# A fused LayerNorm and GELU on one core: the last row's store moved from the hand-written section to a Tile DMA behind it

## Chip, core and metric

One core of a Trainium2 chip. The metric is the device time of one execution in microseconds (us), the median of several runs; lower is better. The profile of one execution comes beside it.

## The reference, cut

```python
def reference(x, gamma, beta, eps):            # x: 8 x 1024 x 2048 float32
    mean = np.mean(x, axis=-1, keepdims=True)
    var = np.var(x, axis=-1, keepdims=True)
    out = gamma * (x - mean) / np.sqrt(var + eps) + beta
    return (0.5 * out * (1 + np.tanh(np.sqrt(2 / np.pi) * (out + 0.044715 * out ** 3)))).astype(np.float32)
```

67 MB come in and 67 MB go out; there is no other large traffic.

## The kernel before

The 8192 rows of 2048 are cut into 16 batches (B) of 128 partitions by 4 rows (R). From here on "a row" of a batch is one of these 4, that is 128 rows of x, one per partition, 1 MB. Five buffers `xts` hold batches in flight. Within one section, `tile_critical`, every engine has its own block and its own semaphores: SyncE (SP) loads batches, VectorE (DVE) takes statistics and scales by gamma, GpSimd (POOL) takes the power for the standard deviation, TensorE adds beta in PSUM, ScalarE (ACT) normalises, applies GELU in place and issues the stores. ACT stores a whole batch at a time, but the last batch row by row, so that its first rows do not wait for the fourth.

```python
    def by_row(b):
        return b == B - 1
    def stored(b):                      # count of the slot's store semaphore before batch b
        return sum(16 * (R if by_row(c) else 1) for c in range(b) if slot(c) == slot(b))

    with tc.tile_critical(no_gpsimd_drain=True):
        with nc.Block(no_gpsimd_drain=True) as block:
            ...
            @block.scalar
            def _(ac):
                ...
                for t in range(T + 1):
                    ...                                     # normalise tile t into yks
                    ins = ac.activation(out=xt[:, q], in_=pss[i % 2], func=ACT.Gelu_apprx_tanh)._wait_ge(s_t, i + 1)
                    if by_row(b):
                        ins.then_inc(s_r, 1)
                        ac.dma_start(out=og[b, :, q:q + 1], in_=xt[:, q:q + 1])._wait_ge(
                            s_r, b + q + 1).then_inc(s_store[slot(b)], 16)
                        ac.sem_inc(s_g, 1)
                    ...
        # still in the section: GpSimd waits for every store
        for b in range(B, B + SLOTS):
            nc.gpsimd.wait_ge(s_store[slot(b)], stored(b))
```

Behind the block stands a barrier of all engines, then GpSimd's waits, then the exit of the section, then the two closing handshakes of the program.

Of the kernel before, what the change touches and what calls it, by code (L numbers as in the profile page):

```python
# [10 lines left out]
R = 4  # L11
# [5 lines left out]
def kernel(  # L17
# [8 lines left out]
    nc = tc.nc  # L26
# [7 lines left out]
    T = n // P  # L34
    B = T // R
    assert (B - 1) % SLOTS == 0
    xg = xf.rearrange("(b p r) d -> b p r d", p=P, r=R)
    og = of.rearrange("(b p r) d -> b p r d", p=P, r=R)
# [7 lines left out]
    def sb(name, shape, dt):  # L46
        return pool.tile(shape, dt, name=name)

    xts = [sb(f"xt{s}", [P, R, d], f32) for s in range(SLOTS)]
# [17 lines left out]
    def sem(name):  # L67
        return tc.alloc_semaphore(name)
# [3 lines left out]
    s_store = [sem(f"store{s}") for s in range(SLOTS)]  # L72
# [15 lines left out]
    def slot(b):  # L88
        return (b + SLOTS - 1) % SLOTS

    def row(p):
        return rows[p:p + 1, :, :d // K]

    def split(v):
        return v.rearrange("o (k f) -> o k f", k=K)
# [4 lines left out]
    def by_row(b):  # L100
        return b == B - 1

    def stored(b):
# [5 lines that stand above are left out]
            @block.sync  # L109
            def _(sy):  # L110
                for b in range(B):
                    s = slot(b)
                    if stored(b):
                        sy.wait_ge(s_store[s], stored(b))
                    for q in range(R):
                        if b == 0:
                            sy.dma_start(out=xts[s][:, q:q + 1], in_=xg[0, :, q:q + 1]).then_inc(s_first[q], 16)
                    if b:
                        sy.dma_start(out=xts[s], in_=xg[b]).then_inc(s_load[s], 16)
# [68 lines left out]
            @block.scalar  # L188
            def _(ac):
                ac.preload_act_table(ACT.Gelu_apprx_tanh)  # L190
                for k, (p, src) in enumerate(((64, gamma), (0, beta), (32, beta))):
                    ac.dma_start(out=row(p), in_=src.rearrange("(o k f) -> o k f", o=1, k=K)).then_inc(s_par[k], 16)
                ac.wait_ge(s_m, 1)
                ac.activation(out=split(b_hl[0:1]), in_=row(0), func=ACT.Identity)._wait_ge(s_par[1], 16).then_inc(s_c, 1)  # L194
                ac.activation(out=split(b_hl[32:33]), in_=row(32),  # L195
                              func=ACT.Identity)._wait_ge(s_par[2], 16).then_inc(s_c, 1)
                ac.activation(out=g_t, in_=pss[0], func=ACT.Identity)._wait_ge(s_tg, 1).then_inc(s_c, 1)  # L197
                for t in range(T + 1):
                    if t < T:
                        b, q = divmod(t, R)  # L200
                        ac.activation(out=yks[t % 2], in_=xts[slot(b)][:, q], func=ACT.Identity, scale=rss[:, q:q + 1],  # L201
                                      bias=nms[:, q:q + 1])._wait_ge(s_p, t + 1).then_inc(s_n, 1)
                    i = t - 1
                    if i < 0:
                        continue
                    b, q = divmod(i, R)
                    xt = xts[slot(b)]
                    ins = ac.activation(out=xt[:, q], in_=pss[i % 2], func=ACT.Gelu_apprx_tanh)._wait_ge(s_t, i + 1)  # L208
                    if by_row(b):
                        ins.then_inc(s_r, 1)  # L210
                        ac.dma_start(out=og[b, :, q:q + 1], in_=xt[:, q:q + 1])._wait_ge(  # L211
                            s_r, b + q + 1).then_inc(s_store[slot(b)], 16)
                        ac.sem_inc(s_g, 1)
                    elif q == R - 1:
                        ins.then_inc(s_r, 1)
                        ac.dma_start(out=og[b], in_=xt)._wait_ge(s_r, b + 1).then_inc(s_store[slot(b)], 16)  # L216
                        ac.sem_inc(s_g, 1)
                    else:
                        ins.then_inc(s_g, 1)
# [29 lines left out]
                    pe.sem_inc(s_z, -R)  # L249


        for b in range(B, B + SLOTS):
            nc.gpsimd.wait_ge(s_store[slot(b)], stored(b))


# [1 line left out]
_INS = ['x', 'gamma', 'beta', 'eps']  # L257
_OUTS = [((8, 1024, 2048), 'float32')]
# [30 lines left out]
```

## Time and profile before

| what | value | where read |
|---|---|---|
| median time | 319.69 us, 3 runs, 319.49 to 319.76 | timing |
| span of the profiled execution | 317.8 us | head of the page |
| busiest compute engine | DVE, 265.0 us, 83% | part 1 of the page |
| DMA engines, loads and stores | 49.4% + 49.1% | part 3 of the page |
| last activation ends | 305.29 us | timeline |
| last store issued / landed | 305.32 / 316.50 us | trace |
| from last landing to the end | 1.29 us | difference to the span |

The digits of the DMA row are tenths of all 16 DMA engines' time in 1/40 of the span: a row of nines next to TensorE, ScalarE and VectorE at 77 to 83% (GpSimd 25%) says that the transfers set the pace. "PEq", "ACTq", "POOLq" and "SPq" are an engine's sequencer, where waits, no-ops, branches and issues of DMA stand; they are not counted as busy. A store has "landed" with the last of its 16 semaphore increments; a "ring" is what one DMA engine still has to do for one queue; a "straggler" is a DMA engine that is late against the others. The lines themselves are in the prediction.

### The profile page before, as it was taken

Reading aid. Unit: us, or ns where it says so; the run is one execution under the profiler, and the core shown is the slowest. Engines: PE = TensorE matmul, PEld = TensorE weight load, DVE = VectorE, ACT = ScalarE, POOL = GpSimd, SP = SyncE. Lnnn points to the kernel's source line nnn. Section 1 sums busy time; section 2 is a strip of 40 time slices with the busy share of each in tenths; the row PEclk is TensorE's granted clock in tenths of the full one; section 3 lists DMA queues with packets and bytes.
Section 4 is the critical chain, followed back from the end, with each engine's and each line's share of the span. In section 5 each row is a group of like instructions: output and inputs, shape, how many; then the busy total and the mean of one; then the engine's idle time right before and its main releaser. Section 6 shows DMA issues by size and latency. Waiting matters only on the chain.

```text
span 317.8 us, 2075 instructions
## 1 busy us (share of the span) xinstructions
PE 244.3 (77%) x520; PEld 57.1 (18%) x520; DVE 265.0 (83%) x514; ACT 253.9 (80%) x132; POOL 79.0 (25%) x73
## 2 busy tenths in 40 slices
PE   2769988888888898888877868598595895868810
PEld 1211222111212122211111111122121111112100
DVE  3499999999999999999969799696996969879500
ACT  2679999999999999999969779696995969968920
POOL 1033323232323231323213222231312213212000
DMA  7999999999999999999999999999999999999994
GB/s 291 438 462 396 459 396 445 412 454 404 458 400 459 422 437 445 412 450 408 458 417 441 437 421 454 404 458 412 450 433 425 450 408 450 408 458 421 437 404 206
DMA packets 5571, 134.27 MB, mean 423 GB/s; under 512 B 656, under 2 KB 704, under 8 KB 704
## 3 DMA queue, kind: packets, MB, share of 16 engines
q1 hardware_dynamic: 2736, 67.11, 49.4%
q10 hardware_dynamic: 2832, 67.13, 49.1%
q14 instruction: 3, 0.02, 0.0%
HBM read 67.13 MB, written 67.11 MB: 422 GB/s over the span
## 4 chain that ended last, share of the span: by engine, by line
DMA 44%; DVE 27%; ACT 19%; PE 3%; issue 2%; ACTq 1%; DVEq 0%; SPq 0%
DMA out_dram<-xt 27%; DVE sts L148 15%; DMA xt<-in_x_dram 15%; ACT yk L201 12%; DVE zg L164 9%; ACT xt L208 7%; PE ps L226 2%; DMA rows<-in_gamma_dram 2%; DVE mvs L157 2%; DVE nms L141 1%; ACTq L216 1%; DVE ves L158 1%; PE ps L243 1%; ACT g_t L197 1%; ACTq L211 0%
## 5 line engine op out<-in xcount | busy, mean ns | idle before, releaser
L148 DVE BATCH_NORM_STATS2 sts<-xt 128x6 f32<-128x512 f32 x256 | 163.5, 681 | 23.7 <-DMA xt<-in_x_dram 21.7
L201 ACT ACTIVATE yk<-xt,nms,rss 128x2048 bf16<-128x2048 f32 x64 | 134.1, 2095 | 41.7 <-DVE nms L141 41.2
L243 PE MATMUL ps<-zg,ident 128*128 128x512 bf16 x256 | 120.8, 627 | 50.9 <-DVE zg L164 50.9
L132 POOL TENSOR_TENSOR rss<-ves,mhalf 128x1 f32<-128x1 f32 x64 | 78.0, 1219 | 216.5 <-DVE ves L158 157.0
L239 PE MATMUL ps<-b_hl,ones_b 33*128 33x512 bf16 x256 | 120.6, 624 | 2.2 <-PEq L234 2.2
L208 ACT ACTIVATE xt<-ps 128x2048 f32<-128x2048 f32 x64 | 118.8, 1857 | 1.5 <-PE ps L243 1.5
L164 DVE TENSOR_TENSOR zg<-yk,g_t 128x2048 bf16<-128x2048 bf16 x64 | 78.0, 1218 | 5.0 <-ACT yk L201 3.0
L243 PEld LDWEIGHTS ps<-zg,ident 128*128 128x128 bf16 x256 | 27.6, 130 | 144.1 <-DVE zg L164 108.7
L239 PEld LDWEIGHTS ps<-b_hl,ones_b 33*128 33x128 bf16 x256 | 27.0, 127 | 92.1 <-issue 88.4
L157 DVE BATCH_NORM_AGGREGATE mvs<-sts 128x2 f32<-128x24 f32 x64 | 16.9, 264 | 2.2
L141 DVE TENSOR_SCALAR nms<-mvs,rss 128x1 f32<-128x1 f32 x64 | 12.6, 196 | 0.0
L226 PE MATMUL ps<-rows,ones 1*128 1x512 f32 x8 | 7.2, 1072 | 6.0 <-DMA rows<-in_gamma_dram 6.0
L158 DVE TENSOR_SCALAR ves<-mvs 128x1 f32<-128x1 f32 x64 | 9.8, 154 | 2.2
L194 ACT ACTIVATE b_hl<-rows 1x2048 bf16<-1x2048 f32 x1 | 1.9, 1909 | 4.9 <-DMA rows<-in_beta_dram 4.9
L226 PEld LDWEIGHTS ps<-rows,ones 1*128 1x128 f32 x8 | 2.5, 323 | 9.2 <-DMA rows<-in_gamma_dram 6.0
L172 DVE TENSOR_TENSOR b_hl<-rows,b_hl 1x2048 bf16<-1x2048 f32 x1 | 2.3, 2281 | 2.1 <-ACT b_hl L195 2.1
L197 ACT ACTIVATE g_t<-ps 128x2048 bf16<-128x2048 f32 x1 | 1.9, 1877 | 2.4 <-PE ps L226 2.4
L190 ACT ACT_TABLE_LOAD x1 | 1.3, 1283 | 0.9 <-SPq L106 0.9
L167 DVE MEMSET b_hl<- 33x1024 uint32 x1 | 0.9, 912 | 1.2 <-SPq L106 1.2
L195 ACT ACTIVATE b_hl<-rows 1x2048 bf16<-1x2048 f32 x1 | 1.9, 1908 | 0.0
L123 POOL MEMSET ones<- 65x128 f32 x1 | 0.2, 202 | 0.5 <-SPq L106 0.5
L127 POOL TENSOR_SCALAR_AFFINE_SELECT ident<-ident 128x128 bf16<-128x128 bf16 x1 | 0.3, 294 | 0.1
(7 smaller groups left out, 0.9 us busy)
## 6 DMA issues: line engine op xcount, KB each, us to landing
xt<-in_x_dram SPq DMA_DIRECT2D x15, 4096.0 KB, 24.3
out_dram<-xt ACTq DMA_DIRECT2D x15, 4096.0 KB, 37.0
xt<-in_x_dram SPq DMA_DIRECT2D x4, 1024.0 KB, 8.1
out_dram<-xt ACTq DMA_DIRECT2D x4, 1024.0 KB, 12.7
rows<-in_beta_dram ACTq DMA_DIRECT2D x2, 8.0 KB, 5.6
rows<-in_gamma_dram ACTq DMA_DIRECT2D x1, 8.0 KB, 5.0
```

The costliest lines, as they stand in the source:

```text
L132: po.tensor_tensor(out=rss[:, c], in0=ves[:, c], in1=mhalf, op=ALU.pow)._wait_ge(s_a, k + 1).then_inc(s_q, 1)
L141: ve.tensor_scalar(out=nms[:, c], in0=mvs[:, q, 0:1], scalar1=rss[:, c], scalar2=-1.0, op0=ALU.mult, op1=ALU.mult)._wait_ge(s_q, count).th ...
L148: ins = ve.bn_stats(out=sts[:, q, j, :], in_=xr[:, j, :])
L157: ve.bn_aggr(out=mvs[:, q], in_=sts[:, q])._wait_ge(s_o, count + 1).then_inc(s_o, 1)
L158: ve.tensor_scalar(out=ves[:, q:q + 1], in0=mvs[:, q, 1:2], scalar1=float(eps), scalar2=1.0, op0=ALU.add, op1=ALU.mult)._wait_ge(s_o, coun ...
L164: ve.tensor_tensor(out=zgs[q % 2], in0=yks[q % 2], in1=g_t, op=ALU.mult)._wait_ge(s_n, count).then_inc(s_z, 1)
L197: ac.activation(out=g_t, in_=pss[0], func=ACT.Identity)._wait_ge(s_tg, 1).then_inc(s_c, 1)
L201: ac.activation(out=yks[t % 2], in_=xts[slot(b)][:, q], func=ACT.Identity, scale=rss[:, q:q + 1], bias=nms[:, q:q + 1])._wait_ge(s_p, t + ...
L208: ins = ac.activation(out=xt[:, q], in_=pss[i % 2], func=ACT.Gelu_apprx_tanh)._wait_ge(s_t, i + 1)
L226: ins = pe.matmul(pss[0][:, cols(j)], lhsT=ones[64:65], rhs=rows[64:65, j * K // nsub:(j + 1) * K // nsub, :d // K], start=True, stop=True)
L239: ins = pe.matmul(ps[:, cols(j)], lhsT=ones_b, rhs=b_hl[:, cols(j)], start=True, stop=False)
L243: ins = pe.matmul(ps[:, cols(j)], lhsT=ident, rhs=zgs[k % 2][:, cols(j)], start=False, stop=True)
```

## The change

The last row's store leaves ACT's block. It becomes an ordinary Tile DMA behind the section, where Tile waits for the section and for the store by itself. GpSimd's wait for all other stores goes into a second section behind that DMA, so that the DMA does not have to wait for them. The intent is to let Tile keep the books of the last store, and to leave the block without issuing it.

```diff
@@ in ACT's block
                     ins = ac.activation(out=xt[:, q], in_=pss[i % 2], func=ACT.Gelu_apprx_tanh)._wait_ge(s_t, i + 1)
+                    if i == T - 1:
+                        continue
                     if by_row(b):
@@ behind the block
+    nc.scalar.dma_start(out=og[B - 1, :, R - 1:], in_=xts[slot(B - 1)][:, R - 1:])
+
+    with tc.tile_critical(no_gpsimd_drain=True):
+
         for b in range(B, B + SLOTS):
-            nc.gpsimd.wait_ge(s_store[slot(b)], stored(b))
+            nc.gpsimd.wait_ge(s_store[slot(b)], stored(b) - (16 if slot(b) == slot(B - 1) else 0))
```

## The prediction

> **What bounds the kernel now.** I read the page first, its occupancy slices and DMA part, because the change moves one store and I must know whether stores are what the end waits for.
>
> ```profile
> DMA  7999999999999999999999999999999999999994
> GB/s 291 438 462 396 459 396 445 412 454 404 458 400 459 422 437 445 412 450 408 458 417 441 437 421 454 404 458 412 450 433 425 450 408 450 408 458 421 437 404 206
> ...
> q1 hardware_dynamic: 2736, 67.11, 49.4%
> q10 hardware_dynamic: 2832, 67.13, 49.1%
> ```
>
> The DMA row is at 9 from the second slice to the last but one. Loads (q1) and stores (q10) take 49.4 and 49.1% of all 16 engines' time, together 98.5%. No compute engine is above 83%. The kernel is bound by moving 134 MB; work beside the transfers costs nothing as long as the DMA engines always have a descriptor waiting. Second I cut the end of the execution into windows (columns: window, its length, busy time of PE, PEld, DVE, ACT, POOL with counts, PE clock, DMA share, GB/s).
>
> ```profile
> 304.00:306.00 2.00, 0.00 (x0) 0.00 (x0) 0.00 (x0) 1.29 (x1) 0.00 (x0) 1.00 0.97 410
> 306.00:308.00 2.00, 0.00 (x0) 0.00 (x0) 0.00 (x0) 0.00 (x0) 0.00 (x0) 1.00 0.99 418
> 308.00:310.00 2.00, 0.00 (x0) 0.00 (x0) 0.00 (x0) 0.00 (x0) 0.00 (x0) 1.00 1.03 434
> 310.00:311.20 1.20, 0.00 (x0) 0.00 (x0) 0.00 (x0) 0.00 (x0) 0.00 (x0) 1.00 1.04 437
> 311.20:313.60 2.40, 0.00 (x0) 0.00 (x0) 0.00 (x0) 0.00 (x0) 0.00 (x0) 1.00 0.90 379
> 313.60:316.10 2.50, 0.00 (x0) 0.00 (x0) 0.00 (x0) 0.00 (x0) 0.00 (x0) 1.00 0.12 52
> 316.10:317.80 1.70, 0.00 (x0) 0.00 (x0) 0.00 (x0) 0.00 (x0) 0.00 (x0) 1.00 0.00 0
> ```
>
> All compute is over at 305.3. From 304 to about 313.6 the engines still run near full on stores already queued. From 313.6 to 316.1 the share is 0.12, that is 2 of 16 engines (2/16 = 0.125): two stragglers, one whole row behind the other fourteen. Then 1.7 us without transfers. Third, the timeline shows the last compute and the last store's issue, and the views of the store's line, of the GpSimd wait, and of the end's own lines show what follows (durations in ns as min/median/max; then first and last start in us).
>
> ```profile
> 303.41 1.88 ACT L208 ACTIVATE xt<-ps 128x2048 f32<-128x2048 f32 x1 [1.48 <-PE ps L243]
> 305.32 0.34 ACTq L211 DMA_DIRECT2D out_dram<-xt  x1
> ```
>
> ```profile
> L211 ACTq DMA_DIRECT2D out_dram<-xt x4: 338/338/338, 293.3 to 305.3; - x4
> ...
> DMA to landing us min/median/max: 11.2/12.7/15.5
> ```
>
> ```profile
> L253 POOLq EVENT_SEMAPHORE  x2: 42/42/43, 306.7 to 316.5; - x2
> ```
>
> ```profile
> L106 POOLq COMPARE_BRANCH  x1: 38/38/38, 316.6 to 316.6; - x1
> L106 POOLq NOP  x1: 13/13/13, 316.8 to 316.8; - x1
> ```
>
> ```profile
> L284 POOLq EVENT_SEMAPHORE  x4: 17/17/17, 317.0 to 317.7; - x4
> L284 POOLq DRAIN  x3: 39/41/97, 316.9 to 317.5; - x3
> ```
>
> The last row is issued at 305.32 and, being the quickest of the four rows to land, takes 11.2 us: 305.3 + 11.2 = 316.5, which is when GpSimd's wait on the stores passes. Then follow a branch (316.6), a no-op (316.8), a drain (316.9) and two handshakes of all engines (317.0 to 317.7); the span ends at 317.8. So from the last landing to the end is 317.8 - 316.5 = 1.3 us, and the whole run (319.6 timed beside this profile) has 1.8 us outside the span, which the change does not touch.
>
> **What the Trainium skill says.** "DMA: Bandwidth & Descriptors", section "Queues, rings and completion order": on each DMA engine the descriptors of one queue are consumed in ring order. All four last rows are on ACT's queue, so the last one must queue behind the third. The trace agrees: four equal 1 MB rows land 15.5 down to 11.2 us after issue, though they are issued some 4.3 us apart and compete with no loads after 280. The same page, "Why a DMA increments its semaphore by 16 and not by 1": the count is full only when the slowest engine has landed. The trace agrees: the wait passed at 316.5, after the two stragglers stopped (316.1), not at 313.6. "Perfetto Trace Analysis", on HWDGE DMA instructions: the recorded time is that of the issuing sequencer, and the movement of data is not in it. Here each row's issue is 338 ns, its landing over 11 us later. So a later issue record is not in itself a later landing.
>
> **The change part by part.** I built both and compared the order of the instructions. All loads, all compute and the first 18 stores are the same on every engine. Four things differ.
>
> (1) The last row's store leaves ACT's block. ACT's drain at the end of the block no longer stands behind a 0.34 us issue and a semaphore increment. Before, it started at 305.77 and ACT reported to the barrier at 305.91; the last activation ends at 305.29, so ACT should now report at about 305.35, 0.55 us sooner.
>
> (2) The same store (same tile, shape and ACT queue) is issued after the section is left: it waits for the block's barrier and for SyncE's collecting no-op. Before, ACT's report at 305.91 led to GpSimd's release (306.02 to 306.04), SyncE's signal (306.13), the other engines' drains (306.2) and SyncE's last collecting wait, ended 306.37: 0.46 us; a no-op and a signal add about 0.1 (a step on these sequencers is 0.04 to 0.08). GpSimd, which no longer waits for stores there, reports in time. So the issue moves from 305.32 to about 305.35 + 0.55 = 305.9, later by 0.6 us, and ends near 306.25.
>
> (3) Is that on the path? The stragglers' rings are busy with the third row until 313.6, the other fourteen until about 311.2 (one row, 2.4 us, before 313.6). The shortest transfer of the page, 8 KB of gamma, issued by the same engine, needs 5.0 us from issue to landing; taken as an upper bound of an issue's start-up, descriptors would be ready at 305.9 + 5.0 = 310.9, still before 311.2 and 2.7 us before 313.6. The delay is absorbed: no bytes are added, no ring runs dry, and the last landing stays at 316.5. Cost 0.
>
> (4) The end. Before, behind the last landing on the path: GpSimd wait, branch, no-op, SyncE's no-op, two drains of SyncE, GpSimd's collecting wait at 316.99. After: GpSimd waits for the earlier stores long before (the three earlier rows of the last slot have all landed by about 314, when the stragglers turn to the last row), and its last wait holds the new store's semaphore. Then come a branch (it carries a wait as before, so 0.17 us for it and the next fetch), a semaphore increment, and two no-ops, each waiting for GpSimd's own signal, then the drain. Steps of 0.08 us: wait 316.53, branch 316.61, increment 316.78, no-ops 316.86 and 316.94, drain 317.02, collecting wait 317.10. SyncE, which waits for the new store itself, is released by the first no-op: wait 316.90, drains 316.97 and 317.03, so it is not later than GpSimd. 317.10 against 316.99 is +0.1 us. The two handshakes behind it are unchanged.
>
> Sum: 0 (issue) + 0.1 (exit) = +0.1 us: 319.69 + 0.1 = 319.8 us; span 317.9.
>
> **The rivals.** *The late issue is exposed.* If the rings ran dry or a late doorbell left a gap, all of the delay would show: +0.6 us, 320.3 to 320.4, or a little more. For it: nothing but the end of the kernel is left to hide it. Against: the windows show 0.97 to 1.04 through 311.2.
>
> *The second section costs a full exit of its own.* If entering and leaving it made all five engines meet again behind the landing, as the first exit does, about another 0.6 us would come, the distance from one such handshake to the next (317.1 to 317.7): 320.4. Against: in the built program only GpSimd passes the second section, and all its waits but the last are satisfied before the landing; the other engines go straight to the final barrier.
>
> *A code fetch stalls at the tail.* The new blocks could lie beyond what is already loaded for GpSimd or SyncE; the page has only three instruction packets and I can't see from it what one miss costs. My estimate is one small transfer's 5.0 us at most, giving 324.8, still inside 2%; GpSimd and SyncE sit idle for 10 us there, so I give it little.
>
> *It gains.* If the wait for the last store was dear because it stood inside the section, the gain could be at most a part of the 1.3 us between landing and end, so 318.4 at the very best. Against: the same steps still follow the landing, with two more.
>
> **Range and chances.** Before's three runs lie within 0.27 us; a different execution may differ by a few tenths more. The mechanisms give +0.1 with exposed rivals up to +0.7. I take 319.8, with 319.2 to 320.5. Two per cent is 6.4 us. No saving of that size exists, since the whole tail behind the last landing is 1.3 us and the bytes stay; a loss of that size would need a stall longer than any rival's. So faster 0.01, within 2% 0.97, slower 0.02.
>
> **What would show it right or wrong.** Right: the ACT issue of the new store's line starts near 305.9, some 0.6 us after the activation's end; it takes about 10.6 us to land instead of 11.2, so the landing is again at about 316.5; the windows keep a share near 1 up to 311.2 and 0.12 from 313.6; the last GpSimd wait is at 316.5 and the span 317.9. The first step is wrong if the issue is past 307; the third if the share falls below 0.9 between 306 and 311 or the landing moves with the issue; the fourth if the distance from landing to end leaves 1.3 to 1.5 us. The prediction is wrong as a whole if the loads or stores before 300 us shift, which I hold to be untouched.

## The result and the profile after

Changed: 320.03 us median of 6 runs (319.97 to 320.37). Before, on the same chip and in the same rounds: 319.73 us (319.46 to 319.98). The ratio is 1.0012 with a 95% interval of 0.9999 to 1.0025. (A ratio is the mean time of one kernel's fast runs over that of the other's of the same rounds, so it is not quite the ratio of the two medians.) By the 2% rule the two are the same, and the interval still holds 1.

The windows of the changed kernel, with the same columns as in the prediction:

```profile
304.00:306.00 2.00, 0.00 (x0) 0.00 (x0) 0.00 (x0) 1.34 (x1) 0.00 (x0) 1.00 0.97 410
306.00:308.00 2.00, 0.00 (x0) 0.00 (x0) 0.00 (x0) 0.00 (x0) 0.00 (x0) 1.00 0.99 418
...
311.20:313.60 2.40, 0.00 (x0) 0.00 (x0) 0.00 (x0) 0.00 (x0) 0.00 (x0) 1.00 0.95 403
313.60:316.10 2.50, 0.00 (x0) 0.00 (x0) 0.00 (x0) 0.00 (x0) 0.00 (x0) 1.00 0.12 49
```

The share stays near 1 while the issue is moved, and the tail of 0.12 is there again: no gap opened. (Its make-up differs. In the packet records before, two engines work to 316.06; in the changed execution one does, to 316.18, and the next two stop at 314.88 and 314.36.) The timeline of the end and the view of the new store's line:

```profile
303.46 1.88 ACT L208 ACTIVATE xt<-ps 128x2048 f32<-128x2048 f32 x1 [1.47 <-PE ps L245]
305.96 0.34 ACTq L254 DMA_DIRECT2D out_dram<-xt  x1
```

```profile
L254 ACTq DMA_DIRECT2D out_dram<-xt x1: 338/338/338, 306.0 to 306.0; - x1
...
DMA to landing us min/median/max: 10.7/10.7/10.7
```

The issue is at 305.96 (0.64 us later than before) and the landing 10.7 us behind it instead of 11.2: at 316.64, against 316.50. Now the lines of the second section and of the program's end:

```profile
L256 POOLq NOP  x3: 13/13/13, 306.0 to 317.1; - x3
L256 POOLq EVENT_SEMAPHORE  x1: 17/17/17, 316.9 to 316.9; - x1
```

```profile
L288 POOLq EVENT_SEMAPHORE  x10: 17/30/8090, 306.1 to 318.0; - x10
L288 SPq EVENT_SEMAPHORE  x4: 17/17/387, 306.0 to 318.0; - x4
```

A new increment of GpSimd's stands at 316.9 and its last new no-op at 317.1, behind the landing: these are the added steps. The two long durations, 8090 ns on GpSimd and 387 ns on SyncE, are no work. They belong to wait instructions that hold two semaphores, and their record starts when the one named first is satisfied: GpSimd's, from 306.13 to 314.22, for ACT's signal (at once) and then for the three earlier rows; SyncE's, from 316.65 to 317.04, for the new store and then for GpSimd. The kernel before has the opposite case: its last wait names the last batch's stores first and a semaphore that was long satisfied second, and its record is 43 ns, at 316.53.

GpSimd's steps behind the landing, start times from the trace: before, landing 316.50, wait 316.53, branch 316.61, no-op 316.78, drain 316.86, collecting wait 316.99. After, landing 316.64, wait 316.66, branch 316.75, increment 316.90, no-ops 317.00 and 317.09, drain 317.14, collecting wait 317.23. From landing to the collecting wait that is 0.48 and 0.59 us; from there to the end 0.81 and 0.83, the clearing of semaphores taking 0.244 us instead of 0.226.

So the span grew from 317.80 to 318.06, by 0.27 us: 0.13 us of it behind the landing (1.29 to 1.42), 0.14 us because the landing itself came later. (The prediction and the expectations have 1.30 for the 1.29, from rounded times.)

### The profile page after: what moved, and what is told of

Its sections match the earlier page's. It is cut to its first block, busy times and chain, and to the rows that moved or that the text cites. A ratio compares the mean times of both kernels' runs of the same rounds, so it can differ in the third digit from the quotient of the medians.

```text
span 318.1 us, 2084 instructions
## 1 busy us (share of the span) xinstructions
PE 244.4 (77%) x520; PEld 57.3 (18%) x520; DVE 265.1 (83%) x514; ACT 253.9 (80%) x132; POOL 79.0 (25%) x73
## 4 chain that ended last, share of the span: by engine, by line
DMA 44%; DVE 27%; ACT 19%; PE 3%; issue 2%; ACTq 1%; DVEq 0%; SPq 0%
DMA out_dram<-xt 26%; DMA xt<-in_x_dram 16%; DVE sts L148 15%; ACT yk L201 12%; DVE zg L164 9%; ACT xt L208 7%; PE ps L228 2%; DMA rows<-in_gamma_dram 2%; DVE mvs L157 2%; DVE nms L141 1%; ACTq L218 1%; DVE ves L158 1%; PE ps L245 1%; ACT g_t L197 1%; ACTq L213 0%
```

## The experiments

Ten kernels ran, on four chips, all correct. "Issue" is the start of the last store's issue (of the last piece where it is cut), "landing" the last increment of any store's semaphore; the last two columns say what follows. The times are medians, with the ratio to the kernel before, run beside them (319.63 to 319.69 us).

| kernel | issue | landing | landing to end | span | median us | ratio (95%) |
|---|---|---|---|---|---|---|
| before | 305.32 | 316.50 | 1.29 | 317.80 | 319.73 | |
| changed | 305.96 | 316.64 | 1.42 | 318.06 | 320.03 | 1.0012 (0.9999 to 1.0025) |
| exit_alone | 306.30 | 316.37 | 1.74 | 318.10 | 320.16 | 1.0016 (1.0003 to 1.0030) |
| last_first | 305.81 | 316.47 | 1.21 | 317.68 | 319.46 | 0.9994 (0.9977 to 1.0012) |
| sections | 306.85 | 316.62 | 5.27 | 321.89 | 323.83 | 1.0131 (1.0116 to 1.0147) |
| late2 | 309.64 | 316.61 | 1.43 | 318.04 | 320.09 | 1.0013 (0.9998 to 1.0028) |
| late4 | 313.46 | 317.36 | 1.43 | 318.80 | 321.23 | 1.0056 (1.0040 to 1.0071) |
| late5 | 315.47 | 319.39 | 1.43 | 320.82 | 322.93 | 1.0113 (1.0096 to 1.0131) |
| wait_first | 314.46 | 318.32 | 1.00 | 319.32 | 321.39 | 1.0053 (1.0038 to 1.0069) |
| sync_queue | 305.95 | 316.87 | 1.73 | 318.60 | 320.49 | 1.0024 (1.0008 to 1.0039) |
| split | 305.94 | 317.24 | 1.29 | 318.53 | 320.39 | 1.0030 (1.0016 to 1.0043) |
| relieve | 307.31 | 317.83 | 1.29 | 319.12 | 321.40 | 1.0065 (1.0052 to 1.0079) |

### Is a later issue a later landing? Three doses of delay

The changed kernel, with activations into a scratch tile on ACT behind the last real one, so that ACT reports to the barrier later and the Tile store is issued later.

```diff
+    junk = sb("junk", [P, d], bf16)
+    s_j = tc.alloc_semaphore("j")
...
                     if i == T - 1:
+                        for k in range(2):        # 4 and 5 in the other two
+                            ac.activation(out=junk, in_=xts[slot(0)][:, 0], func=ACT.Identity)._wait_ge(s_j, k).then_inc(s_j, 1)
                         continue
```

Two more activations:

> The changed kernel with two more activations (128x2048, about 2 us each, into a scratch tile) on ACT after the last real one, so that the Tile store is issued some 4 us later, near 310. My theory (the rings of the slowest DMA engines are busy with the third row until 313.6, and an issue needs about 1 us until its first packet, as the first load of the trace shows: issued 0.94, first packet 1.95): last landing stays at 316.5 to 316.7, time 320.0. Rival (a later issue is a later landing): +4 us, 324.

```profile
L258 ACTq DMA_DIRECT2D out_dram<-xt x1: 338/338/338, 309.6 to 309.6; - x1
...
DMA to landing us min/median/max: 7.0/7.0/7.0
```

The issue is 3.7 us later than in the changed kernel, the time from issue to landing 3.7 us shorter, and the landing is at 316.61: fully absorbed. 320.09 us against 320.03. The rival that a later issue is a later landing is out.

Five more:

> The same with five more activations, issue near 316, past the point (313.6 - 1.0 = 312.6) where the slowest rings run dry. My theory: the landing is then issue + 1.0 + one row at 2.45 us + 0.45 from the last packet to the semaphore, 316 + 3.9 = 319.9, that is +3.3 us against the changed kernel: about 323.3. Rival (delay shows one to one): +10 us, 330. Rival (the store is hidden whatever its issue): 320.

```profile
L258 ACTq DMA_DIRECT2D out_dram<-xt x1: 338/338/338, 315.5 to 315.5; - x1
...
DMA to landing us min/median/max: 3.9/3.9/3.9
```

Its windows at the end:

```profile
311.20:313.60 2.40, 0.00 (x0) 0.00 (x0) 0.00 (x0) 2.37 (x2) 0.00 (x0) 1.00 0.14 58
313.60:316.10 2.50, 0.00 (x0) 0.00 (x0) 0.00 (x0) 1.24 (x1) 0.00 (x0) 1.00 0.00 0
316.10:319.10 3.00, 0.00 (x0) 0.00 (x0) 0.00 (x0) 0.00 (x0) 0.00 (x0) 1.00 0.85 350
```

Here the delay shows: the share falls to 0.14 while only the stragglers move the third row, to 0.00 in the next window, and returns when the late row arrives. The landing is 3.9 us behind the issue, as expected. I had put the issue at 316; the activations took 1.93 us each, not 2, and it came at 315.47, hence 322.93 us instead of 323.3. A delay of 9.5 us cost 2.75 us of landing.

Four more, to look just past the point where it should begin:

> The changed kernel with four more activations before the last row's store, so the issue is near 305.96 + 4 x 1.94 - 0.2 = 313.5, just past the point where it should begin to show. From the runs so far, a store issued to idle rings lands 3.9 us after its issue (issue 315.47, landing 319.39; issue 314.46, landing 318.32), and a store issued before 312.7 should be hidden behind the slowest engine (316.6). My theory: landing at 313.5 + 3.9 = 317.4, time 320.0 + 0.8 = 320.8 to 320.9. Rival (the delay is hidden until all rings are empty at 314.2): 320.0. Rival (a gap in the rings costs a restart beyond the 3.9): above 321.5.

```profile
L258 ACTq DMA_DIRECT2D out_dram<-xt x1: 338/338/338, 313.5 to 313.5; - x1
...
DMA to landing us min/median/max: 3.9/3.9/3.9
```

Issue 313.46, landing 317.36, again 3.9 us apart. The expected 317.4 is met. The median of 321.23 is above the expected 320.8 to 320.9, because two of the four runs are at 320.86 and 320.91 and two at 321.55 and 321.76; the profiled one is the lowest. The two high runs lie in the range of the rival of a restart (above 321.5) and left no trace: for the profiled execution that rival is out, for them it is not tested.

Together with the changed kernel and the next one, five points obey one rule: the landing is the later of 316.6 and the issue plus 3.9 us. The bend at 312.7 is worked out from it; no run was issued between 309.64 and 313.46. The issue of the changed kernel, 305.96, is 6.7 us ahead of the bend.

### What if there were no second section?

The other form that the change could have had: the Tile store stands behind the first section, and GpSimd's wait for the other stores stays in that section.

```diff
+                    if i == T - 1:
+                        continue
...
         for b in range(B, B + SLOTS):
-            nc.gpsimd.wait_ge(s_store[slot(b)], stored(b))
+            nc.gpsimd.wait_ge(s_store[slot(b)], stored(b) - (16 if slot(b) == slot(B - 1) else 0))

+    nc.scalar.dma_start(out=og[B - 1, :, R - 1:], in_=xts[slot(B - 1)][:, R - 1:])
```

> The Tile store without a second section: GpSimd's wait for all other stores stays in the first section, so the Tile store is issued only after the third row has landed everywhere. My theory: GpSimd passes at about 314.0 to 314.2, the issue is at about 314.4, all 16 engines start together at 315.4, last landing at 314.4 + 3.9 = 318.3; the exit is shorter because no GpSimd step follows (about 1.1 instead of 1.42): end 319.4, against 318.1 of the changed kernel: +1.3 us, time about 321.3. Rival (the place of the wait does not matter because the bytes are the same): 320.0.

```profile
L258 ACTq DMA_DIRECT2D out_dram<-xt x1: 338/338/338, 314.5 to 314.5; - x1
...
DMA to landing us min/median/max: 3.9/3.9/3.9
```

```profile
L256 POOLq EVENT_SEMAPHORE  x2: 43/43/43, 306.9 to 314.1; - x2
```

GpSimd's wait passes at 314.13 and the store is issued at 314.46, so it begins with empty rings. 321.39 us against the expected 321.3. This is what the second section is for: it takes the wait for the other stores from in front of the last one. (Its exit of 1.00 us is the shortest of all, because SyncE alone waits for the last store; the late landing costs more than that gives.)

### What does the second section itself cost?

First the second half of the change alone: the last row's store stays in ACT's block, and GpSimd's waits go into a second section.

```diff
+    with tc.tile_critical(no_gpsimd_drain=True):
+
         for b in range(B, B + SLOTS):
             nc.gpsimd.wait_ge(s_store[slot(b)], stored(b))
```

> Second half of the change alone: the last row's store stays in ACT's block as before, and the wait for all stores moves from the first section into a second one on GpSimd. My theory (only GpSimd's own steps behind the last landing count, some 0.08 us each): issue at 305.3, last landing at 316.5 as before, and the path from landing to end grows from 1.30 us, by more than in the changed kernel (1.42), because here the built order puts the last slot's wait first and four satisfied waits behind it: 1.30 + 0.12 + 4 x 0.085 = about 1.75 us, so +0.45 us, 320.1 to 320.2. Rival 1 (the second section costs a full meeting of all engines, about 0.6 us, in whatever order): 1.9 or more, also in the changed kernel, which already speaks against it. Rival 2 (the late issue, not the exit, is what the changed kernel pays for): no difference from before, 319.7.

In the built program the last slot's wait is the first of five, where in the changed kernel the new store's is the last.

```profile
L286 POOLq EVENT_SEMAPHORE  x9: 17/43/8867, 307.5 to 318.0; - x9
...
L286 POOLq COMPARE_BRANCH  x2: 33/36/38, 0.8 to 316.8; - x2
```

The 8867 ns wait ended at 316.39, four satisfied waits followed at 316.44, 316.53, 316.62 and 316.70, and the branch out of the section was at 316.79. From landing to end it took 1.74 us, against 1.75 expected. The late issue can't be the reason: the store is in the block as before. (Its issue, 306.30, is later than before's only because all of ACT's last work came 1 us later in this execution; the landing, 316.37, is not later for that.)

Then the cost multiplied: the changed kernel with four more sections, each with a wait that is already satisfied.

```diff
+    for _ in range(4):
+        with tc.tile_critical(no_gpsimd_drain=True):
+            nc.gpsimd.wait_ge(s_store[0], 16)
```

> The changed kernel with four more sections of the second one's kind behind it, each with a wait on GpSimd that is satisfied already. It multiplies the disputed cost of a section behind the last landing. My theory: each adds only GpSimd's own steps, about nine of 0.085 us and a branch's 0.1, so 0.85 us each, 3.4 us for four: landing at 316.6 as before, path from landing to end 1.42 + 3.4 = 4.8 us, time about 323.4. Rival (each section ends with a meeting of all engines): the other engines show extra handshake steps between the sections, and each costs more, 1.3 us or above, 325 or more. Rival (sections are free for waits satisfied): 320.0.

```profile
L262 POOLq NOP  x12: 13/13/13, 317.2 to 320.9; - x12
L262 POOLq EVENT_SEMAPHORE  x4: 17/17/17, 317.8 to 320.7; - x4
```

```profile
L292 ACTq DRAIN  x2: 8/80/152, 307.2 to 321.3; - x2
```

ACT still drains twice, as in the changed kernel, and nothing of it lies between the sections: they are GpSimd's alone. The increments stand at 316.88, 317.76, 318.63 and 319.49, 0.86 to 0.88 us apart, as expected. The fourth added section took 1.24 us: two no-ops, 319.68 and 320.14, start 0.46 us apart instead of 0.09. Its cause stays open (this trace has no instruction packet, queue q14, between 108 and 320.8 us); it makes 0.37 us of the difference between the expected 3.4 and the measured 3.85 us.

Last, the smallest lever: the kernel before with its five waits written in the opposite order.

```diff
-        for b in range(B, B + SLOTS):
+        for b in range(B + SLOTS - 1, B - 1, -1):
```

> The kernel before with GpSimd's five waits written in the opposite order, nothing else. In the built program the first wait written is the one that is carried by the branch out of the section, so the last slot's wait moves from the second of two wait instructions onto the branch. If the exit is the sum of GpSimd's steps behind the last landing, one step of 0.085 us goes: from landing to end 1.21 instead of 1.30 us, time lower by less than 0.1 us, which the timing can't tell from 319.7. If the order of the waits is of no matter: 1.30.

```profile
L253 POOLq EVENT_SEMAPHORE  x2: 43/43/43, 306.6 to 306.7; - x2
```

```profile
L106 POOLq COMPARE_BRANCH  x1: 38/38/38, 316.5 to 316.5; - x1
```

Both wait instructions are now over at 306.7 and the branch itself waits for the last landing (316.47) and passes at 316.50. From landing to end: 1.21 us, one step less. It is the only version below both kernels in span, and the timing can't show it: 319.46 us, ratio 0.9994 (0.9977 to 1.0012).

### What ends the stores?

The changed kernel with the Tile store issued by SyncE, that is, in the other queue:

```diff
-    nc.scalar.dma_start(out=og[B - 1, :, R - 1:], in_=xts[slot(B - 1)][:, R - 1:])
+    nc.sync.dma_start(out=og[B - 1, :, R - 1:], in_=xts[slot(B - 1)][:, R - 1:])
```

> The changed kernel with the Tile store issued by SyncE instead of ACT, so that it stands in the other queue and shares the DMA engines with the three earlier rows instead of standing behind them. My theory (the end is set by the bytes that the slowest engine still has to move, not by the order within ACT's queue): issue near 306.0, the last row itself lands earlier than the third or with it, the last landing of all stays at 316.5 to 316.7. GpSimd's wait for the last slot, which is followed by four more waits, may now be the last to pass, which costs up to 4 x 0.085 us more: 320.0 to 320.4. Rival (the ring order behind ACT's rows is what costs the time): the end comes 2 us or more earlier, 318 or less.

```profile
L254 SPq DMA_DIRECT2D out_dram<-xt x1: 347/347/347, 305.9 to 305.9; - x1
...
DMA to landing us min/median/max: 8.8/8.8/8.8
```

The last row no longer stands behind the third: it landed at 314.73, 8.8 us behind its issue, and the third row landed last, at 316.87. The order changed and the end did not come sooner: the sum of what the slowest engine has to move counts. GpSimd's wait for the third row now passed last, with four more behind it, and the exit grew to 1.73 us, close to exit_alone's 1.74. 320.49 us, 0.1 above the expected range.

Two kernels tried to use that sum, cutting the last row of the kernel before into pieces that, by the Trainium skill's rule (its place is named in the first expectation), go to fewer engines. GpSimd's count of the stores is raised to match; that line is left out of the cuts.

```diff
+                        cut = 120 if q == R - 1 else P
-                        ac.dma_start(out=og[b, :, q:q + 1], in_=xt[:, q:q + 1])._wait_ge(
+                        ac.dma_start(out=og[b, :cut, q:q + 1], in_=xt[:cut, q:q + 1])._wait_ge(
                             s_r, b + q + 1).then_inc(s_store[slot(b)], 16)
+                        if cut < P:
+                            ac.dma_start(out=og[b, cut:, q:q + 1], in_=xt[cut:, q:q + 1]).then_inc(s_store[slot(b)], 16)
```

> The kernel before, with the last row's store cut into one of 120 partitions and one of 8. The Trainium skill (DMA: Bandwidth & Descriptors, Why a DMA increments its semaphore by 16 and not by 1) says that 120 partitions go to the 15 lowest engines and 8 partitions to the 8 lowest. If the one straggler, or the later of the two, is the highest engine, it has no last row to store and is done by 313.7 to 314.2; the others have 8 or 9 packets of 0.306 us and land at 314.3 to 314.6: 2 us sooner, 317.7. If a straggler is among the lowest 8, it has 9 packets: landing 316.8, 320.0. If it is between, no change, 319.7. It tests the theory that what ends the kernel is the one or two engines a row behind.

```profile
L256 POOLq EVENT_SEMAPHORE  x2: 43/43/43, 307.0 to 317.3; - x2
```

The wait passed at 317.26, 0.73 us later than before's 316.53. That is the direction of the case "a straggler is among the lowest 8", but more than its one packet of 0.306 us. The packet records, followed from end to start, give the rest: the engine that ends last does move nine packets, but it turns to the last row at 314.14 instead of 313.60, 0.53 us later, after a packet of the third row that took 604 ns instead of 309; and its last packet is followed by the landing after 0.34 instead of 0.45 us. Why that packet took so long is not known.

```diff
-                        ac.dma_start(out=og[b, :, q:q + 1], in_=xt[:, q:q + 1])._wait_ge(
-                            s_r, b + q + 1).then_inc(s_store[slot(b)], 16)
+                        cuts = (0, 80, 115, 122, P) if q == R - 1 else (0, P)
+                        ac.wait_ge(s_r, b + q + 1)
+                        for lo, hi in zip(cuts, cuts[1:]):
+                            ac.dma_start(out=og[b, lo:hi, q:q + 1], in_=xt[lo:hi, q:q + 1]).then_inc(s_store[slot(b)], 16)
```

> The kernel before, with the last row cut into stores of 80, 35, 7 and 6 partitions. By the Trainium skill's rule for the number of engines (the largest number up to 16 that divides the partitions, on the lowest engines) these use 16, 7, 7 and 6 engines, so that the seven lowest engines move 11 or 12 packets of the last row and the nine others 5 instead of 8. The cut of 120 and 8 made the end later (landing 317.2), so a straggler is among the lowest eight; the skill's table names engine 7 as usually slow, with 15. If the stragglers are above the lowest seven: they end at 313.7 + 5 x 0.306 + 0.45 = 315.7, the lowest seven at 311.3 + 12 x 0.306 + 0.5 = 315.5: landing 0.8 us sooner, 318.9. If one is among the lowest seven: 12 packets after 313.6, landing 317.8 or later, 321 or more. If stragglers do not set the end: 319.7.

```profile
L255 POOLq EVENT_SEMAPHORE  x2: 43/43/43, 308.6 to 317.9; - x2
```

The hoped gain turned into a loss: landing 317.83, 1.33 us later than before, against 4 more packets of 0.306 us = 1.22 us for an engine with 12 instead of 8. That fits stragglers among the lowest engines, which both cuts loaded further; and the two engines that end last here, at 317.33 and 317.37, each show the completions of the pieces 0.31 us apart, the pattern of an engine that moves all four pieces. The issues of the pieces took longer, up to 0.98 us, but were over at 308.03, before any ring could need them (311.2). Both cuts failed as improvements; as tests they agree with the reading that the end is set by one or two engines that are a row behind. The trace does not name the engine of a packet, so which ones they are rests on the skill's rule.

## Why the prediction was right

The time lay within the range (320.03 in 319.2 to 320.5), the class was right, and the mechanism stands step by step.

- *The issue moves to about 305.9.* Measured 305.96. The reckoning from the old trace's steps (0.55 us earlier report of ACT, 0.55 us from there to the issue) held to 0.06 us: ACT reported at 305.43, 0.08 later than reckoned, and the issue followed after 0.54.
- *The delay is absorbed.* Shown by late2, in which 3.7 us more changed the landing by 0.03 us, and bounded by late4, late5 and wait_first. The prediction used the 5.0 us of a small load as a cautious bound of the start-up; a whole row on empty rings needs 3.9 us, so the slack was larger than it dared to say: 6.7 us.
- *The exit costs +0.1 us.* Measured +0.13: 0.11 in GpSimd's steps, where it was predicted, and 0.02 in the clearing of semaphores.
- *The landing stays at 316.5.* Measured 316.64. This term was set at 0 and came out at +0.14 us, more than half of the measured +0.27 in span. The issue does not explain it: the store of the batch before, issued at 288.90 and 288.96 and with a semaphore of its own, had landed 0.14 us later too, at 306.84 instead of 306.71, and it stands four rows ahead of the moved store's end. In the six executions with the last row unsplit, on ACT's queue and ahead of the bend, the last landing follows that one by 9.80 to 9.87 us, close to four rows of 2.45 us each, whatever the issue: it is the backlog of the slowest engine, and the +0.14 was already in it. Over all twelve traces that earlier landing is at 306.50 to 306.72 in the five kernels without the Tile store and at 306.74 to 307.10 in the seven with it, so it seems to belong to the program's form. By what way, no run shows.
- *The rivals.* An exposed issue (+0.6 us) is refuted by late2. A section that makes all engines meet is refuted by the sections run: ACT has no step between them. The gain of up to 1.3 us did not come. A fetch that stalls was not seen in the changed kernel, whose trace has no instruction packet behind 109 us; nothing in the trace of the sections run ties its unexplained 0.37 us to one either.

Three readings in the prediction were loose. It let the three earlier rows be landed by about 314; GpSimd's wait for them ended at 314.22. Before, all four rows share one semaphore, so the trace of before does not tell which row an increment near 314 belongs to, and of the 15.5 to 11.2 us to landing only the last row's 11.2 is sure. The rows are not all "some 4.3 us apart": the last is issued 3.35 us behind the third. And its sign of being wrong as a whole, a shift of loads or stores before 300 us, came by the letter: single loads are issued up to 1.74 us earlier (120.15 to 118.41). But exit_alone and last_first, which have no Tile store, have that load at 118.38 and 118.36, and the last load ends at 279.63 before and 279.65 after, so it is a spread between executions.

## What to carry to other kernels

Ask of a delayed store not how late it is issued but how much work its DMA engines still have: here a delay cost nothing until issue plus 3.9 us passed the landing that the slowest engine's backlog allowed. What stands behind the last landing is paid in full, so count the steps there, and put the wait that ends last where the fewest instructions follow it: the place of the last wait among the five was worth 0.09 us (last_first against before) to 0.31 us (exit_alone against changed) behind the landing. A wait in front of a store was dear here because it outlasted the backlog (issue 314.46, behind the bend at 312.7); to avoid that is what the second section was for.

## What the Trainium skill lacked or had wrong

- "DMA: Bandwidth & Descriptors", "Latency and other measured facts", calls DMA engines 7 and 15 usually slow and, as a best guess, ties it to the descriptor rings of the GpSimd path. Here no DMA is issued by GpSimd, and still one or two of 16 engines trail by a row (share 0.12 for 2.5 us). By the same page's rule for the number of engines, the cut that gave 12 packets only to the six lowest ended 1.33 us later, close to four packets; that does not fit 7 or 15 as the slow ones.
- The same table gives about 600 ns to the first byte for issues from SyncE and ACT. On empty rings the first packet of the late store started 0.85 us behind the start of the issue (315.47 to 316.32 in late5), and the whole 1 MB row took 3.9 us to land.
- "Perfetto Trace Analysis", "Sequencer-only Instruction (DRAIN, etc)", says that the recorded start is when all semaphores are satisfied. For a wait on two semaphores the record began when the one named first was satisfied: 8090 ns on GpSimd and 387 ns on SyncE, nearly all of it waiting.
- No page that was looked up gives the cost of a sequencer's satisfied wait or no-op on GpSimd, 0.087 and 0.094 us each, or of a section that only GpSimd passes, 0.86 to 0.88 us.
